# A hand-written list of small moves in the issue order of TensorE, ScalarE and VectorE, for a GLA and RWKV-7 inference step

## The chip, the cores and the metric

One core of one Trainium2 chip runs the whole program. The metric is device time in microseconds (us), the median of several executions. The engines are TensorE (PE; its weight loads are shown apart as PEld), VectorE (DVE), ScalarE (ACT), GpSimd (POOL) and SyncE (SP), which issues every DMA of this kernel. Each engine works through its own list of instructions in order, and waits on semaphores for the others.

## The reference

One layer of a hybrid decoder, for a prompt of 1024 tokens and for 8 single-token samples with stored states, width 1024, float32. Cut to what matters:

```python
p = einsum('btd,dn->btn', x, w_in)                    # one wide projection: GLA, RWKV and gate columns
# GLA branch, 4 heads: S_t = diag(a_t) S_{t-1} + k_t^T v_t ; o_t = q_t S_t   (chunked)
o_gla, S_gla = _gla_chunked(q, k, v, log_a, S_gla0)   # then RMS norm per head and a silu gate
# RWKV-7 branch, 16 heads of 64, per token:
# S_t = S_{t-1} (diag(w_t) - kk_t^T (kk_t * a_t)) + v_t^T k_t ; y_t = S_t r_t
y, S_rwkv = _rwkv7_scan(r, w, k, v, kk, a, S_rwkv0)   # then group norm, bonus term and a silu gate
m = sigmoid(gate_a) * (o_gla @ w_up_gla) + sigmoid(gate_b) * (o_rwkv @ w_up_rwkv)
y_out = layernorm(2**0.25 * x + m @ w_out)
```

It also returns both branches' states and the last projected row.

## The kernel before

The prompt is taken in two passes of 512 tokens; the first pass carries the 8 samples along. In each pass blocks of 128 columns of `w_in` are multiplied with x. A float32 product is made of three reduced-precision matmuls: weight and x are each split into a rounded part and a remainder (`wpart` and `xh`, `xl`), so that a block is 8 x 3 matmuls into a PSUM tile `proj` (the three `yield self.P.matmul(...)` in `blocks`). ScalarE or VectorE rounds a loaded weight piece (`CAST wpart<-wraw`), VectorE makes the remainder in the first pass; the second pass reads both kinds again from memory.

Between these blocks stand the two branches, each a generator that yields one operation at a time:

- `pair`: two RWKV heads at a time, eight per pass. `front` makes decays and products on ScalarE and VectorE; among the VectorE work are four half-height multiplies into the tile BK (rows `wide<-row 64x512`) and one `scalar_tensor_tensor` (r x rk x k), whose result `head_sums` splits into two `part` tiles and sums over each head with `headsr` on TensorE. After them come a triangular inverse on GpSimd (tiles X, Xt), and `back`, which assembles inverse blocks with four 32x32 transposes into `Xd` on VectorE and two groups of narrow matmuls, `big<-Xd,Ld` and `big<-Yd,Xt`, on quarters of the array.
- `chain`: the eight chunks of 64 tokens of a pair in sequence. Each chunk has three small float32 matmuls into the single bank `pch`: `pch<-wide,gg`, then `rh` (a copy) and `pch<-rh,XT`, a copy into u, then `pch<-wide`, and two 64x65 additions on VectorE (`wide<-pch,gg`, one for each head) that make the next chunk's u.
- `gla_head`: a GLA head (rows `big<-row ...`, narrow groups on 64x64 tiles among them, the copy S, the running state).

At the end come the two up-projections, the merge, the output product and the layer norm.

The order is not written by hand. `Order.run` keeps a model of five engines' times, and at each step takes the operation that can start first by it, less a priority (`PRIO`, `FOR_PE`, `TUNED`); the moment it is chosen, `op.fn()` issues it on its engine. Tiles are taken from pools (`take`) and given back (`free`) in the same order. Nearly all instructions are issued through `make` in class `Engine`, so that they all bear the line of its lambda (L283 in the profile of before, L316 after the change); the tiles tell them apart.

Of the kernel before, what the change touches and what calls it, by code (L numbers as in the profile page):

```python
# [20 lines left out]
P = 128  # L21
# [75 lines left out]
URGENT = 1.952  # L97

BOUNCED = (0, 1)

STRETCH = 5
TUNED = {
# [37 lines left out]
SIGMOID, EXP = "sigmoid_and_others", "natural_log_exp_and_others"  # L140
# [45 lines left out]
class Op:  # L186


    def __init__(self, ways, out, ins, lag=0.0, table=None, tiles=None, port=""):
        self.ways, self.out, self.ins, self.lag, self.table, self.tiles = ways, out, ins, lag, table, tiles  # L190
        self.port, self.outs = port, [out]
        self.eng, self.fn, self.cost = ways[0]
# [123 lines left out]
class Order:  # L316
# [4 lines left out]
    def __init__(self, nc):  # L321
        self.P, self.A, self.V, self.G, self.S, self.E, self.C = (Engine(**e) for e in (
            {"P": nc.tensor}, {"A": nc.scalar}, {"V": nc.vector}, {"G": nc.gpsimd}, {"S": nc.sync},
            {"V": nc.vector, "G": nc.gpsimd}, {"A": nc.scalar, "V": nc.vector}))
        self.tiles = (P, P)
        self.quads = {"V": {}, "A": {}}
        self.time = dict.fromkeys("PAVGS", 0.0)
        self.port = dict.fromkeys("VG", 0.0)
        self.dma = 0.0
        self.flight = [0.0] * FLIGHT  # L330
        self.table = EXP
        self.ready, self.read = {}, {}
        self.streams, self.stretch = [], None
        self.tune(0)
        self.idle, self.make, self.home, self.wait = {}, {}, {}, {}
        self.kept, self.tile = {}, {}

    def tune(self, n):
# [4 lines left out]
            self.for_pe = {k: max(0.0, FOR_PE.get(k, 0.0) + x.get("pe " + k, 0.0)) for k in PRIO}  # L343

    def buffers(self, tag, bufs, make):
        self.idle[tag], self.make[tag], self.wait[tag] = [0.0] * bufs, make, 0

    def fixed(self, tag, tiles):

# [19 lines left out]
    def take(self, tag):  # L369
        idle = self.idle[tag]  # L370
        t = min(idle)
        idle.remove(t)
        x = self.make[tag]()
        self.home[x.tensor.name] = tag
        if tag in self.kept:
            self.tile[x.tensor.name] = x
        self.ready[x.tensor.name] = (t, None)
        return x

    def free(self, *xs):  # L380
        for x in xs:
            n = x.tensor.name
            tag = self.home.pop(n)
            self.idle[tag].append(max(self.ready.pop(n)[0], self.read.pop(n, 0.0)))
            if tag in self.kept:
                self.kept[tag].append(self.tile.pop(n))

# [60 lines left out]
    def run(self):  # L448
        while self.streams:
            best, before = None, list(self.streams)  # L450
            self.urgent = self.needed()
            stand = max(STAND, SCARCE - PER_ROW * len(self.idle["row"]))
            for s in before:
                self.advance(s)
                if s.op is not None:
                    t = self.start(s.op)
                    if s.op.eng == "P":
                        key = t - stand * self.for_pe[s.kind] - (SWITCH if s.op.tiles != self.tiles else 0.0)
                    else:
                        key = t - self.prio[s.kind]  # L460
                    if s.kind in self.urgent:
                        key -= URGENT
                    if s.op.table not in (None, self.table):
                        key += max(0.0, TABLE - AGE * s.op.late)
                    if best is None or key < best[0]:
                        best = key, t, s
            if best is None:
                assert self.streams != before, "streams wait for one another"
                continue
            _, t, s = best  # L470
            op, s.op = s.op, None
            cost = op.cost
            if op.table not in (None, self.table):
                cost += TABLE
                self.table = op.table
                self.nc.scalar.preload_act_table_set(self.table)  # L476
            op.fn()
            self.time[op.eng] = max(self.time[op.eng], t + cost)
            if op.eng in op.port:
                self.port[op.eng] = t + cost  # L480
            if op.eng == "P":
                self.tiles = op.tiles
            elif op.eng in "VA":
                for x, q in self.starts(op):
                    self.quads[op.eng][x is op.out, x.space] = q
            end = t + cost
            if op.eng == "S":
                self.dma = max(self.dma, end) + op.lag[0]
                end = self.dma + op.lag[1]
                self.flight.append(end - EARLY)  # L490
            for x in op.outs:
                n = x.tensor.name
                self.ready[n] = max(end, self.ready.get(n, (0.0,))[0]), "D" if op.eng == "S" else op.eng
            for x in op.ins:
                n = x.tensor.name
                self.read[n] = max(self.read.get(n, 0.0), end)


class Kern(Order):
# [344 lines left out]
    def first_blocks(self, xs):  # L844

        run = []
        for b in self.plan[:2]:
            evac = yield from b.act()
            for tt, (t0, n) in enumerate(b.c.tiles):
                ps = yield from self.get("big")  # L850
                run.append((b, tt, t0, n, ps, evac))
        w, idle = {}, (yield from self.bank("pch", [P, P]))
        half = len(run) // 2
        for k, part in [(0, run[:half]), (1, run[:half]), (0, run[half:]), (1, run[half:])] + [(k, run) for k in range(2, NK)]:
            yield lambda: len(xs) > k
            for b, tt, t0, n, ps, evac in part:
                f0 = t0 - LEAD if b.lead and tt else t0
                q = ps[:, :t0 + n - f0]
                if tt == 0 and k % 4 == 0:
                    yield lambda: self.ws  # L860
                    w[id(b)] = self.ws.pop(0)
                hi, lo = (w[id(b)][:, v, k % 4 * P:k % 4 * P + P] for v in range(2))
                xh, xl = xs[k]
                yield self.P.matmul(q, hi, xh[:, f0:t0 + n], start=(k == 0), stop=False)
                yield self.P.matmul(q, hi, xl[:, f0:t0 + n], start=False, stop=False)
                yield self.P.matmul(q, lo, xh[:, f0:t0 + n], start=False, stop=(k == NK - 1))
                fin = tt == len(b.c.tiles) - 1
                if fin and k % 4 == 3:
                    yield from self.used(w[id(b)])
                if k == NK - 1:  # L870
                    self.spawn(self.evacuate(evac(tt, t0, n, q), ps, b.post if fin else None), "evacuate")
            for _ in range(IDLE if part is not run and part[0] is run[0] else 0):
                yield self.P.matmul(idle, self.warm, self.warm, start=True, stop=True)
            if k == 2:
                self.free(idle)
# [382 lines left out]
    def front(self, c, p, st, d):  # L1258
# [57 lines left out]
        self.free(ta, tb, te, td, r)  # L1316
        if c.i in BOUNCED:
            d.w = None
# [117 lines left out]
    def turn(self, c, d):  # L1436

        d.u = d.L.rearrange("p (c h v) -> p c h v", c=NCH, h=2)
        if c.i in BOUNCED:
            yield lambda: d.w is not None  # L1440
        m = yield from self.get("vm")
        if c.i in BOUNCED:
            w = d.w.rearrange("p (c v) -> p c v", v=C)
# [567 lines left out]
```

## Time and profile before

| | us |
|---|---|
| median of 3 runs (1435.57 to 1439.01) | 1437.1 |
| the profiled execution's own time | 1436.47 |
| its span, first to last instruction | 1434.7 |
| TensorE busy | 1415.7 |
| TensorE weight loads busy | 1245.6 |
| VectorE busy | 1071.1 |
| ScalarE busy | 871.8 |
| GpSimd busy | 414.1 |

The profiled execution is 0.6 us under the median. A matmul's recorded duration reaches past the start of the next one, since matmuls are pipelined; so the spacing of two starts tells what a matmul costs, and "idle before" in a row of the timeline counts only from the modelled end of the one before it.

### The profile page before, as it was taken

The numbers are of one execution on the slowest core, as the hardware profiler recorded it, in microseconds if no ns is written. First come the engines' busy times: TensorE is split into PE (matmuls) and PEld (weight loads), VectorE is DVE, ScalarE is ACT, GpSimd is POOL, SyncE is SP. The second block draws the span as 40 slices with busy tenths as digits, with TensorE's granted clock in tenths as the row PEclk, the third lists the DMA queues.
The fourth block names the chain that finished last, engine by engine and source line by source line (L and its number), as shares of the span: only waits on it lengthen the run. The fifth ranks groups of instructions, "written<-read, shape, count | busy, mean of one in ns | idle before, by whom it ended". The sixth has DMA issues, their size and how long they took to land.

```text
span 1434.7 us, 30718 instructions
## 1 busy us (share of the span) xinstructions
PE 1415.7 (99%) x10576; PEld 1245.6 (87%) x10576; DVE 1071.1 (75%) x2150; ACT 871.8 (61%) x2149; POOL 414.1 (29%) x1150
## 2 busy tenths in 40 slices
PE   9999999999999999999999999999999999999997
PEld 9999999999999998878788878888878897997786
DVE  7688688859886879563887888978785856676685
ACT  6556766666757667646575746586757655654210
POOL 1060524150624150505243514063414260000000
PEclk9999999999999999999999999999999999999999
DMA  7685977586867785688777778677677598798732
GB/s 262 182 261 149 269 220 218 137 244 202 237 179 209 243 264 173 172 239 245 230 207 210 196 242 215 182 218 214 173 230 228 174 273 260 246 302 284 256 126 81
DMA packets 341911, 310.26 MB, mean 216 GB/s; under 512 B 195411, under 2 KB 210908, under 8 KB 341756
## 3 DMA queue, kind: packets, MB, share of 16 engines
q1 hardware_dynamic: 341756, 308.31, 72.0%
q8 instruction: 84, 1.38, 0.4%
q14 instruction: 71, 0.58, 0.1%
HBM read 214.23 MB, written 92.92 MB: 214 GB/s over the span
## 4 chain that ended last, share of the span: by engine, by line
PE 89%; DVE 5%; ACT 4%; DMA 2%; issue 1%; SPq 0%; DVEq 0%; ACTq 0%
PE proj L283 57%; PE big L283 26%; PE pch L283 6%; ACT row L283 2%; DVE row L283 2%; DVE wide L283 1%; DMA wraw<-w_in 1%; ACT L476 1%; DMA wraw<-w_up_gla 1%; DVE wpart L283 1%; ACT wpart L283 0%; ACT part L283 0%; DVE az L283 0%; PE pch L600 0%; DVE xl L283 0%
## 5 line engine op out<-in xcount | busy, mean ns | idle before, releaser
L283 PE MATMUL proj<-xh,wpart 128*128 128x256 f32 (+3 forms) x3712 | 898.5, 327 | 3.4 <-DVE wpart L283 3.0
L283 PEld LDWEIGHTS proj<-xh,wpart 128*128 128x128 f32 x3712 | 617.2, 188 | 54.2 <-issue 4.6
L283 PE MATMUL proj<-xl,wpart 128*128 128x512 f32 (+3 forms) x1856 | 606.7, 327 | 0.2 <-DVE xl L283 0.2
L283 PEld LDWEIGHTS proj<-xl,wpart 128*128 128x128 f32 x1856 | 349.7, 188 | 26.6 <-issue 3.2
L283 POOL TENSOR_TENSOR Xt<-X,wide 128x60 f32<-128x60 f32 (+24 forms) x496 | 174.5, 352 | 413.5 <-DMA wide<-LD 245.6
L283 ACT CAST wpart<-wraw 128x512 fp32r<-128x512 f32 x298 | 182.3, 618 | 80.8 <-PE proj L283 31.3
L283 POOL TENSOR_TENSOR X<-X,Xt 128x60 f32<-128x60 f32 (+24 forms) x496 | 178.2, 359 | 38.6
L283 DVE TENSOR_TENSOR row<-row 128x512 f32<-128x512 f32 (+8 forms) x338 | 175.6, 530 | 10.2 <-ACT row L283 5.4
L283 DVE TENSOR_TENSOR wpart<-wraw,wpart 128x512 fp32r<-128x512 f32 x208 | 142.6, 696 | 44.5 <-ACT wpart L283 40.0
L283 ACT ACTIVATE row<-row 128x520 f32<-128x520 f32 (+4 forms) x229 | 138.0, 612 | 8.8 <-DMA row<-sg 3.3
L283 PE MATMUL big<-xh,wpart 128*128 128x256 f32 (+3 forms) x560 | 135.6, 328 | 0.4 <-ACT xh L283 0.4
L283 ACT COPY row<-big 128x128 f32<-128x128 f32 (+5 forms) x195 | 62.4, 341 | 65.1 <-PE big L283 61.4
L283 PEld LDWEIGHTS big<-xh,wpart 128*128 128x128 f32 x560 | 94.1, 189 | 8.5 <-ACT xh L283 0.8
L283 POOL TENSOR_TENSOR row<-row 128x512 f32<-128x512 f32 (+5 forms) x31 | 31.6, 1028 | 237.1 <-DVE row L283 116.4
L283 DVE TENSOR_TENSOR wide<-pch,gg 64x65 f32<-64x65 f32 x224 | 49.7, 222 | 63.1 <-PE pch L283 59.9
L283 PE MATMUL big<-xl,wpart 128*128 128x256 f32 (+3 forms) x280 | 91.4, 326 | 0.5 <-DVE xl L283 0.5
L283 ACT COPY rh<-pch 128x130 f32<-128x130 f32 x126 | 33.8, 268 | 95.2 <-PE pch L283 94.7
L283 DVE SCALAR_TENSOR_TENSOR row<-proj,pv,row 128x255 f32<-128x255 f32 (+1 forms) x95 | 54.4, 572 | 41.0 <-ACT tail L283 29.5
L283 ACT COPY wide<-pch 64x65 f32<-64x65 f32 x242 | 50.2, 207 | 42.2 <-PE pch L283 37.7
L283 PE MATMUL big<-row 128*64 128x64 f32 (+5 forms) x680 | 68.8, 287 | 0.0
L283 ACT ACTIVATE row<-proj,omu 128x256 f32<-128x256 f32 (+1 forms) x95 | 51.7, 545 | 26.6 <-PE proj L283 25.9
L476 ACT ACT_TABLE_LOAD x52 | 66.7, 1283 | 0.8
(221 smaller groups left out, 2049.5 us busy)
## 6 DMA issues: line engine op xcount, KB each, us to landing
wraw<-w_in SPq DMA_DIRECT2D x292, 256.0 KB
w<-wpart SPq DMA_DIRECT2D x146, 256.0 KB
wpart<-w SPq DMA_DIRECT2D x146, 256.0 KB
wide<-LD SPq DMA_DIRECT2D x64, 128.0 KB
BT<-row SPq DMA_DIRECT2D x32, 256.0 KB
wide<-BT SPq DMA_DIRECT2D x64, 128.0 KB
wraw<-w_up_gla SPq DMA_DIRECT2D x32, 256.0 KB
row<-w_out SPq DMA_DIRECT2D x32, 256.0 KB
```

What stands on the lines that cost most here:

```text
L283: ways.append((eng, lambda call=call: call(out, *args, **kw), price(eng, name, out, args, ins)))
L476: self.nc.scalar.preload_act_table_set(self.table)
```

## The change

The planner still runs as before, on the same numbers. But instead of issuing an operation when it chooses it, it appends it to a list (engine, function, tiles written, tiles read, activation table). For each tile taken from a pool it also notes which tile held that place before (`gone`, `follows`). When the plan is done, `issue` works out from the tiles which operations each one needs, makes one list for each engine, applies the table `MOVES` to the lists of TensorE ("P", 104 entries), ScalarE ("A", 58) and VectorE ("V", 99), and issues everything: always the operation that was planned earliest among those that stand first on their engine and have all they need issued. An entry (n, d) takes the operation at place n of its engine's list and puts it d places later (earlier where d is negative); entries apply one after the other. Without entries the issued program is that of before, instruction for instruction, with the same waits. The lists of GpSimd and SyncE have no entries, so the DMAs stand in the same order as before. No operation is added or removed, and the number of activation-table loads is the same (53).

```diff
+MOVES = {"P": [
+    (6, -4), (12, -2), (15, -4), (13, 2), (336, 9), (336, 8), (345, -1), (747, 4), (874, 3), (874, 5), (898, -11),
...
     def take(self, tag):
         idle = self.idle[tag]
         t = min(idle)
+        before = self.gone[tag].pop(idle.index(t))
         idle.remove(t)
         x = self.make[tag]()
+        self.follows[x.tensor.name] = before
...
-                self.nc.scalar.preload_act_table_set(self.table)
-            op.fn()
+            self.issued.append((op.eng, op.fn, {x.tensor.name for x in op.outs}, {x.tensor.name for x in op.ins}, op.table))
...
+        self.issue()
+
+    def issue(self):
+
+        todo = {e: [] for e in "PAVGS"}
+        wrote, read, touch, needs = {}, {}, {}, []
+        for n, (eng, _, outs, ins, _) in enumerate(self.issued):
+            todo[eng].append(n)
+            need = {wrote[x] for x in outs | ins if x in wrote}
+            for x in outs | ins:
+                if x in self.follows and x not in touch:
+                    need.update(touch.get(self.follows[x], ()))
+                touch.setdefault(x, []).append(n)
+            for x in outs:
+                need.update(read.pop(x, ()))
+                wrote[x] = n
+            for x in ins - outs:
+                read.setdefault(x, []).append(n)
+            needs.append(need)
+        for eng, moves in MOVES.items():
+            for n, places in moves:
+                todo[eng].insert(n + places, todo[eng].pop(n))
+        loaded, done, at = EXP, set(), dict.fromkeys(todo, 0)
+        while len(done) < len(self.issued):
+            n = min(todo[e][k] for e, k in at.items() if k < len(todo[e]) and needs[todo[e][k]] <= done)
+            eng, fn, _, _, table = self.issued[n]
+            if table not in (None, loaded):
+                loaded = table
+                self.nc.scalar.preload_act_table_set(table)
+            fn()
+            done.add(n)
+            at[eng] += 1
```

Three places show what the entries do. The numbers in the names of tiles differ between the programs, because after the change all tiles are made before the first instruction is issued; where a name is needed to follow, the sentences say which is which.

First, VectorE at 851 to 858 us of the profile of before, in the second pass. `wide_11134<-pch_12527` (after: `wide_1974<-pch_2222`) are a chunk's two additions, `wpart_12407` and `wpart_12506` (after: `wpart_2202` and `wpart_2216`) two weight pieces. Before:

```order
L283 TENSOR_TENSOR wide_11134<-pch_12527,gg_11136 64x65
L283 CAST wpart_12407<-wraw_12415 128x512
L283 CAST wpart_12506<-wraw_12511 128x512
L283 TENSOR_TENSOR wide_11134<-pch_12527,gg_11136 64x65
L283 STREAM_TRANSPOSE row_12538<-wide_12062 128x512
L283 SCALAR_TENSOR_TENSOR row_12544<-row_12545,row_12544 128x512
```

And after:

```order
L316 TENSOR_TENSOR wide_1974<-pch_2222,gg_1976 64x65
L316 CAST wpart_2202<-wraw_2204 128x512
L316 TENSOR_TENSOR wide_1974<-pch_2222,gg_1976 64x65
L316 STREAM_TRANSPOSE row_2223<-wide_2131 128x512
L316 CAST wpart_2216<-wraw_2218 128x512
L316 SCALAR_TENSOR_TENSOR row_2225<-row_2226,row_2225 128x512
```

The second cast moved two places later, behind the second addition and a transposition; the first cast still stands between the two additions.

Second, VectorE at 261 to 269 us, in the first pass. `wide_3888` (after: `wide_778`) is BK of a pair, `row_3925<-row_3472` (after: `row_788<-row_723`) the `scalar_tensor_tensor` of its `head_sums`, `part_4241` (after: `part_833`) the second of the two parts, `S_4186` (after: `S_823`) a GLA state. Before:

```order
L283 TENSOR_TENSOR wide_3888<-row_3924,row_3923 64x8x64
L283 STREAM_TRANSPOSE Xd0_184<-XT0_178 32x4x32 x4
L283 TENSOR_TENSOR wide_3888<-row_3585,row_3923 64x8x64
L283 SCALAR_TENSOR_TENSOR row_3925<-row_3472,pv_88,row_3585 128x512
L283 TENSOR_TENSOR wpart_4197<-wraw_4093,wpart_4197 128x512
L283 COPY S_4186<-big_4148 128x256
L283 TENSOR_TENSOR part_4241<-row_3925,part_4240 128x512
```

And after:

```order
L316 TENSOR_TENSOR wide_778<-row_787,row_786 64x8x64
L316 COPY S_823<-big_819 128x256
L316 STREAM_TRANSPOSE Xd0_184<-XT0_178 32x4x32 x2
L316 SCALAR_TENSOR_TENSOR row_788<-row_723,pv_88,row_737 128x512
L316 STREAM_TRANSPOSE Xd0_184<-XT0_178 32x4x32 x2
L316 TENSOR_TENSOR wide_778<-row_737,row_786 64x8x64
L316 TENSOR_TENSOR wpart_826<-wraw_811,wpart_826 128x512
L316 TENSOR_TENSOR part_833<-row_788,part_832 128x512
```

The `scalar_tensor_tensor` moved ahead of a multiply, and together with the copy S ahead of the last two of the four transpositions into Xd.

Third, TensorE at 548 to 552 us, where the pair's two narrow groups (`big<-Xd,Ld` and `big<-Yd,Xt`, 128x32 tiles of the array) and a GLA head's 64x64 products of `row` with itself (128x64 tiles) stand near each other. Before:

```order
L283 MATMUL big_8709<-Xd0_184,Ld_7748 32x128 x4
L283 MATMUL proj_8695<-xh6_317,wpart_8592 128x256
L283 MATMUL big_8740<-part_8684,headsr_154 128x512
L283 MATMUL proj_8695<-xl6_336,wpart_8592 128x256
L283 MATMUL proj_8695<-xh6_317,wpart_8592 128x256
L283 MATMUL proj_8695<-xh7_335,wpart_8592 128x256
L283 MATMUL big_8735<-Yd0_182,Xt_8733 32x128 x4
L283 MATMUL proj_8695<-xl7_384,wpart_8592 128x256
L283 MATMUL proj_8695<-xh7_335,wpart_8592 128x256
L283 MATMUL big_8740<-part_8685,headsr_154 128x512
L283 MATMUL big_8759<-row_7894 64x64 x4
L283 MATMUL big_8759<-row_7896 64x64 x4
```

And after:

```order
L316 MATMUL proj_1539<-xl7_240,wpart_1527 128x256
L316 MATMUL proj_1539<-xh7_234,wpart_1527 128x256
L316 MATMUL big_1548<-part_1537,headsr_154 128x512
L316 MATMUL big_1541<-Xd0_184,Ld_1389 32x128 x4
L316 MATMUL big_1550<-row_1414 64x64 x4
L316 MATMUL big_1550<-row_1416 64x64 x4
L316 MATMUL big_1550<-row_1471 64x64 x4
L316 MATMUL big_1546<-Yd0_182,Xt_1545 32x128 x4
L316 MATMUL proj_1549<-xh0_200,wpart_1522 128x266
```

The first narrow group moved behind the block's remaining matmuls, and the second behind the GLA head's groups: the three stand in one row now, with no full-array matmul between them. Over the whole program the list of TensorE changes the shape of its array tiles 219 times before and 211 times after.

More of the change, by code (lines that the diff above doesn't have):

```diff
@@ L332, in __init__ @@
         self.ready, self.read = {}, {}
-        self.streams, self.stretch = [], None
+        self.streams, self.stretch, self.issued = [], None, []
         self.tune(0)
-        self.idle, self.make, self.home, self.wait = {}, {}, {}, {}
+        self.idle, self.make, self.home, self.wait, self.gone, self.follows = {}, {}, {}, {}, {}, {}
         self.kept, self.tile = {}, {}
@@ L345, in buffers @@
     def buffers(self, tag, bufs, make):
-        self.idle[tag], self.make[tag], self.wait[tag] = [0.0] * bufs, make, 0
+        self.idle[tag], self.make[tag], self.wait[tag], self.gone[tag] = [0.0] * bufs, make, 0, [None] * bufs
     def fixed(self, tag, tiles):
@@ L384, in free @@
             self.idle[tag].append(max(self.ready.pop(n)[0], self.read.pop(n, 0.0)))
+            self.gone[tag].append(n)
             if tag in self.kept:
```

30 rows, old and new, of the table MOVES are left out of this document.

## The prediction

> **What bounds the kernel now.** I read the page's busy times, clock and chain first, then the table by stretches, the waits of TensorE, and at each long wait the timeline of TensorE and of the engine it waited for.
>
> ```profile
> PE 1415.7 (99%) x10576; PEld 1245.6 (87%) x10576; DVE 1071.1 (75%) x2150; ACT 871.8 (61%) x2149; POOL 414.1 (29%) x1150
> ...
> PEclk9999999999999999999999999999999999999999
> ...
> PE 89%; DVE 5%; ACT 4%; DMA 2%; issue 1%; SPq 0%; DVEq 0%; ACTq 0%
> ...
> L283 PEld LDWEIGHTS proj<-xh,wpart 128*128 128x128 f32 x3712 | 617.2, 188 | 54.2 <-issue 4.6
> ```
>
> TensorE is busy 99% of the span at full clock in all 40 slices, and the chain that ended last runs through it for 89%. An order that leaves the instructions as they are can only win what TensorE stands still, and what its changes of form cost. The next rows (busy us of PE, PEld, DVE, ACT, POOL by stretch) bound the first:
>
> ```profile
> 1427.00:1434.70 7.70, 0.01 (x1) 0.00 (x0) 4.38 (x9) 0.50 (x2) 0.00 (x0) 0.72 0.19 68
> sum 1434.70, PE 1415.71 PEld 1245.56 DVE 1071.06 ACT 871.76 POOL 414.06; mean PE 157.30 PEld 138.40 DVE 119.01 ACT 96.86 POOL 46.01
> ```
>
> Of 1434.7 - 1415.7 = 19.0 us without a matmul 7.7 are the tail behind the last one, which the table does not touch. The rest is in TensorE's waits (sum, number, longest):
>
> ```profile
> PE proj L283 <- DVE wpart L283: 3.0, 3, 1.8
> PE big L283 <- ACT part L283: 2.8, 4, 1.0
> PE pch L283 <- DVE wide L283: 1.8, 3, 0.9
> ...
> PE big L283 <- DVE xl L283: 0.5, 2, 0.3
> PE big L283 <- DVE S L283: 0.4, 1, 0.4
> PE proj L283 <- DVE row L283: 0.4, 2, 0.2
> PE big L283 <- ACT xh L283: 0.4, 1, 0.4
> PE proj L283 <- DVE xl L283: 0.2, 1, 0.2
> PE big L283 <- DVE gg L283: 0.2, 1, 0.2
> ```
>
> Eighteen stops, 9.7 us. A stop costs more than its idle time, since that counts only from the modelled end of the matmul before:
>
> ```profile
> 855.86 0.40 PE L283 MATMUL proj<-xl,wpart 128*128 128x512 f32 x1
> 856.09 0.39 PE L283 MATMUL proj<-xh,wpart 128*128 128x512 f32 x1
> 857.37 0.46 PE L283 MATMUL pch<-wide,gg 128*128 128x130 f32 x2 [0.89 <-DVE wide L283]
> ...
> 686.08 0.63 PE L283 MATMUL proj<-xh,wpart 128*128 128x512 f32 x2
> 687.29 0.50 PE L283 MATMUL big<-part,headsr 128*128 128x512 f32 x1 [0.58 <-ACT part L283]
> 687.63 0.40 PE L283 MATMUL proj<-xl,wpart 128*128 128x512 f32 x1
> ```
>
> Undisturbed, 512 columns follow each other every 0.23 us (855.86 to 856.09), so the next was due at 856.32 and came 1.05 late, 0.16 more than the 0.89 shown. Behind a stop the next start comes 0.34 instead of 0.23 later (687.29 to 687.63). I add 0.28 to each stop: all eighteen are worth 9.7 + 18 x 0.28 = 14.7 us, 1% of the time. The Trainium skill, "Perfetto Trace Analysis", section "Identifying the Most-Contended Engine", holds matmul busy time a bad measure of a TensorE's headroom and names the busy share of weight loads instead; by its measure 13% of the span, some 187 us (an estimate from the 87% above), would be open. The pitch of 0.23 decides here: a 512-column matmul outlasts its weight load of 0.188, so weight loads idle there though nothing waits.
>
> **The change, part by part.** No instruction and no DMA is added or dropped; SyncE's and GpSimd's lists stand as they were. So each term is a stop that goes, stays or comes.
>
> (1) The three `pch` stops on VectorE's additions: the additions move ahead of what held them. The rows of VectorE at one of them:
>
> ```profile
> 851.39 0.22 DVE L283 TENSOR_TENSOR wide<-pch,gg 64x65 f32<-64x65 f32 x1 [0.58 <-PE pch L283]
> 853.62 0.44 DVE L283 CAST wpart<-wraw 128x512 fp32r<-128x512 f32 x1 [2.01 <-DMA wraw<-w_in]
> 856.53 0.43 DVE L283 CAST wpart<-wraw 128x512 fp32r<-128x512 f32 x1 [2.47 <-DMA wraw<-w_in]
> 856.99 0.23 DVE L283 TENSOR_TENSOR wide<-pch,gg 64x65 f32<-64x65 f32 x1
> ```
>
> The two additions read the same `pch`. The first ran at 851.39; the second stood behind two casts that waited for their DMAs, until 856.99, and TensorE stopped for it. After the change only the first cast is ahead of it: it ends by 853.62 + 0.44 + 0.23 = 854.3, two us before 856.32. The second cast waits for its DMA as before, behind an addition and a transposition that are done by 855. Gain of the three: 1.8 + 3 x 0.28 = 2.6.
>
> (2) The four stops on `part`, where a pair's `head_sums` waits for its `scalar_tensor_tensor`. The table moves that ahead of multiplies in all four; the rows of VectorE at 687, and TensorE and VectorE at 404:
>
> ```profile
> 684.82 2.43 DVE L283 SCALAR_TENSOR_TENSOR row<-row,pv 128x512 f32<-128x512 f32 x2
> ...
> 404.56 0.50 PE L283 MATMUL big<-part,headsr 128*128 128x512 f32 x1 [0.98 <-ACT part L283]
> ...
> 403.77 1.28 DVE L283 TENSOR_TENSOR wpart<-wraw,wpart 128x512 fp32r<-128x512 f32 x2
> 404.97 0.69 DVE L283 TENSOR_TENSOR part<-row,part 128x512 fp32r<-128x512 f32 x1
> ```
>
> At 687 it passes two multiplies, more than a us of work, and the second `part` is asked for five matmuls later than before: 0.58 + 0.28 = 0.86, all gained. The stop of 0.44 at 829 is alike: 0.72. At 404 the first half comes in time, but the second `part` (404.97 to 405.66) keeps nearly all of VectorE's work ahead of it, only one weight remainder (1.28 / 2 = 0.64) passes behind: 0.64 of the 1.26. The last is the place of the second order piece:
>
> ```profile
> 265.35 0.43 PE L283 MATMUL big<-Xd,Ld 128*32 128x128 f32 x8
> ...
> 268.45 0.50 PE L283 MATMUL big<-part,headsr 128*128 128x512 f32 x1 [0.80 <-ACT part L283]
> ...
> 264.64 0.62 DVE L283 STREAM_TRANSPOSE Xd<-XT 32x128 f32<-32x128 f32 x2
> 265.29 1.69 DVE L283 TENSOR_TENSOR wide<-row 64x512 f32<-64x512 f32 x1
> 267.00 0.75 DVE L283 SCALAR_TENSOR_TENSOR row<-row,pv 128x512 f32<-128x512 f32 x1
> ```
>
> Here the moved 0.75, and the copy S, stand ahead of the last two transpositions, which end at 265.26 before and some 1.2 later now; TensorE needs them at 265.35. The stop of 0.80 goes, one of about 1.1 comes 3 us earlier. I count zero. Together 0.86 + 0.72 + 0.64 = 2.2.
>
> (3) Five small stops have entries at their place: `xh` and one `big` `xl` at 1292 us, where four matmuls of the next tile fill the gap; one `row`, the `proj` `xl`, and `gg`. 0.4 + 0.3 + 0.2 + 0.2 + 0.2 + 5 x 0.28 = 2.7.
>
> (4) What stays: the three `wpart` stops (3.0 + 0.84), since the casts they wait for wait themselves for a DMA (853.62 above), and DMAs keep their order. The `S` stop at 1119 us and the other `xl` and `row` stops at 1133 to 1135 lie in a stretch in which VectorE has no slack:
>
> ```profile
> 1117.00:1134.00 17.00, 16.34 (x118) 12.54 (x117) 16.12 (x27) 13.08 (x30) 5.00 (x3) 1.00 0.62 185
> ...
> 1075.41 0.50 PE L283 MATMUL proj<-xh,wpart 128*128 128x512 f32 x1 [0.97 <-DVE wpart L283]
> ```
>
> It is busy 16.12 of 17.0 us, and no entry carries work out past 1134; a us won at 1119 is waited for again at 1133. Zero.
>
> (5) TensorE's changes of array form, 219 to 211. Rows at the third order piece:
>
> ```profile
> 548.49 0.28 PE L283 MATMUL proj<-xh,wpart 128*128 128x256 f32 x1
> 548.70 0.42 PE L283 MATMUL big<-Xd,Ld 128*32 128x128 f32 x8
> 549.05 0.39 PE L283 MATMUL proj<-xh,wpart 128*128 128x256 f32 x1
> 549.27 0.40 PE L283 MATMUL big<-part,headsr 128*128 128x512 f32 x1
> ```
>
> A 256-column matmul takes 0.12 to the next start in a row of its kind (half of the 0.23 of 512); on the way into the narrow group it is 0.21, and the first one behind the group takes 0.22. A trip out and back costs 0.09 + 0.10 = 0.2. At this place three trips become one; over the program eight changes go: at least 0.8 (each half a trip), at most 8 trips or 1.6, since a change between two narrow forms may cost less than one to and from the full array. I take 1.6: the counts of changes from and to the full array fall by eight each.
>
> (6) New stops. Of the nine places that I followed one by one, one traded its stop for another (268) and one kept half (404). The other two hundred entries are unread; the same may happen there. Two more stops of mean size, 14.7 / 18 = 0.82, make -1.6. Bounds: none, or every gain of (1) to (3) given back, -7.5.
>
> Sum: 2.6 + 2.2 + 2.7 + 1.6 - 1.6 = 7.5 us off the profiled execution's 1436.5, 1429.0. That execution is 0.6 under the median, so for the median 1429.5, 0.5% faster.
>
> **The rivals.** More is won: no new stops, 404 and 268 in full (another 1.7), and the many one-place moves saving something that my stops don't show: 11 to 15 us, 1422 to 1426. The stop at 268, read closely, speaks against it.
>
> Half is given back: VectorE and ScalarE do the same work in total, and where they are dense (1117 to 1134) an earlier operand only means a later other one. 3 to 4 us stay, 1433.5. For it: one in four of the `part` stops already comes to nothing. Against: VectorE is idle a quarter of the span.
>
> Nothing is won: TensorE comes sooner to the weight pieces, and the next late DMA takes back what was gained since the one before. All but what lies behind 1152 us, the last `wpart` stop, would go: 1435 to 1436. Against: a load is issued when TensorE has freed a buffer, so the loads come sooner too.
>
> It is slower: an operation moved forward waits at the head of its engine's list, and holds all behind it, as the two casts above held an addition. At 1075 us an entry puts just such a cast, which TensorE waits for, ahead of a copy out of PSUM. The price of one is the 2.0 to 2.5 us of those casts' waits, if TensorE needs what is behind. To come out slower by 0.2% it takes (7.5 + 2.9) / 2.5, four or five that TensorE feels. The Trainium skill's "TensorE: Matmul & The Clock Gate", section "Architectural detail: the array is 16× 32×32, not 1× 128×128", says that VectorE's and ScalarE's queues are strictly first in, first out. By that rule the trace agrees: the addition of 856.99 had its operand before 851.39 and did not overtake.
>
> **How the numbers follow.** No change means within 0.2% of 1437.1 (2.9 us, what a measurement of this kernel can tell), 1434.2 to 1440. The forecast, 1427 to 1432, has 0.50; more won 0.15; half given back, 1432 to 1434.2, 0.20; nothing won 0.09; slower 0.06. Faster is 0.50 + 0.15 + 0.20 = 0.85. The range from 1423 to 1436 leaves out the slower case, half of the unchanged one and the lower end of the second: below 0.2.
>
> **What would show it.** The page would have TensorE's busy time nearly the same and the span some 7 us shorter. In the waits of TensorE `DVE wide` would be gone and `ACT part` under 1.5, `DVE wpart` still near 3. At the second order piece's place TensorE would wait for the transpositions into Xd instead of for `part`. At the third, the narrow groups would follow each other without a full-array matmul between. I would be wrong if `DVE wpart` grew by what the others lost (nothing won), or if new rows such as `Xd` added up to more than 3 us (given back).

## The result, and the profile after

The changed kernel took 1426.7 us (median of six executions, 1424.0 to 1430.4) beside 1436.5 for the kernel before (median of six, 1435.6 to 1439.0): ratio 0.9933, 95% interval 0.9912 to 0.9954. Run again in the first experiment it came to 0.9948 (0.9934 to 0.9962). So 0.5 to 0.7% is won, 7.5 to 9.7 us; forecast were 7.5. The profiled execution is a long one: 1430.4 us, span 1428.6, 6.1 us shorter than the span before.

The busy times and the chain, the row of the tail (the last 7.9 us, columns as in the stretches of the prediction), and the waits of TensorE:

```profile
PE 1410.7 (99%) x10576; PEld 1245.5 (87%) x10576; DVE 1072.7 (75%) x2150; ACT 870.9 (61%) x2149; POOL 418.2 (29%) x1150
...
PE 89%; DVE 4%; DMA 3%; ACT 2%; issue 1%; SPq 1%; DVEq 0%; ACTq 0%
...
1420.70:1428.60 7.90, 0.22 (x2) 0.02 (x1) 4.37 (x9) 0.50 (x2) 0.00 (x0) 0.75 0.19 66
...
PE proj L316 <- DVE wpart L316: 3.2, 2, 2.5
PE pch L316 <- DVE wide L316: 1.9, 2, 1.3
PE pch L316 <- ACT rh L316: 1.2, 2, 1.0
...
PE big L316 <- DVE part L316: 0.7, 2, 0.5
PE pch L316 <- ACT row L316: 0.6, 1, 0.6
PE big L316 <- issue: 0.3, 1, 0.3
PE big L316 <- DVE gg L316: 0.3, 1, 0.3
PE pch L316 <- ACT wide L316: 0.2, 1, 0.2
PE big L316 <- DVE sto L316: 0.2, 1, 0.2
PE proj L316 <- DVE row L316: 0.2, 1, 0.2
```

The tail is as it was. The waits without the warm-up's 1.1 us fell only from 9.7 to 8.8 us, while the span fell by 6.1: most of the old stops are gone (the four on `part` too; the two stops on `part` that are there now, 0.7 together, are at other places), others have come, and the longest is longer. The rest of the gain lies where this view shows nothing, since TensorE's modelled busy time (1415.7, now 1410.7) covers every delay too short to count as idle.

A view that counts all of it is worked out from the starts of matmuls in the traces: the start of the n-th matmul before, less that of the n-th in the other kernel, is the lead at that place (median over 24 starts). The table has what the lead gained over a stretch of the kernel before; "changed" is the execution above, e1 to e9 are the experiments below:

```
us of before changed   e1    e2    e3    e4    e5    e6    e9
200-212        0.75  0.74  0.73  0.07  0.10  0.08  0.08  0.08
262-275        1.12  1.12 -2.68  1.12 -0.02 -0.04  0.33  1.09
286-300        0.47  0.47  0.48 -0.04 -0.01  0.00 -0.20  0.00
325-345        0.90  0.90  0.55  0.73  0.53  0.50  0.24  0.50
345-375       -1.32 -0.25 -0.74  0.13 -0.66  0.05 -0.03 -0.16
395-416        1.04  1.04 -0.02  0.89  0.22  0.46  0.28  0.61
465-485       -0.80 -0.83 -0.00 -0.80 -0.85  0.00  0.00  0.00
680-691        0.69  0.70 -0.52  0.83  0.09 -0.57  0.47  0.64
700-735       -1.01 -0.49 -0.38 -1.05 -1.68  0.25  0.35 -1.60
820-846        0.68  0.69 -0.35  0.03  0.01  0.01  0.03  0.01
846-862       -1.08  1.49 -0.64  1.49 -1.27  1.11  1.15  1.49
1070-1082     -0.31  0.39  0.15  1.21  0.11 -0.47 -0.47  0.06
1112-1130      0.97  0.97 -0.01  0.97  0.23  0.99 -0.19  0.80
1130-1156      0.10 -0.89 -0.08 -0.31  0.08  0.07 -4.65 -1.02
1156-1175      0.76  0.76 -0.47  0.38  0.76  0.76  0.00  0.79
1232-1245      0.36  0.33  0.36 -0.00  0.36  0.01  0.00  0.00
1280-1300      1.22  1.22  1.22  0.01  0.57  0.00  0.01  0.01
elsewhere      1.55  0.24  0.39  2.66  1.19 -1.07  1.08  0.16
all            6.08  8.60 -2.02  8.32 -0.25  2.12 -1.53  3.45
```

Most steps repeat to 0.03 us in each kernel that has the same entries (262-275, 1112-1130). Others differ between two executions of one program (345-375, 846-862, 1070-1082): there TensorE waits for something behind a transfer. The last row is also the difference of the spans. Cut into stretches of 25 us throughout, the profiled execution won 11.9 us and lost 5.9 again (14.6 and 8.5 in stretches of 10 us, where matmuls that only change places count as well).

The kernel before, too, is here in a single execution, and its own luck stands in every column. e7 and e10 below show how much: e7 has entries at 479 and 693 us only, and "gains" 1.24 at 846-862; e10 moves no matmul and nothing on ScalarE or VectorE, and "gains" 0.59 at 1156-1175. At 1130-1156 the two lose 0.79 and 0.97, with nothing moved there. So the steps at these three places do not by themselves speak for or against an entry.

### The profile page after: what moved, and what is told of

Same layout as the page of the kernel before. It is cut to its first block, busy times and chain, and to the rows that moved or that the text cites. A ratio compares the mean times of both kernels' runs of the same rounds, so it can differ in the third digit from the quotient of the medians.

```text
span 1428.6 us, 30711 instructions
## 1 busy us (share of the span) xinstructions
PE 1410.7 (99%) x10576; PEld 1245.5 (87%) x10576; DVE 1072.7 (75%) x2150; ACT 870.9 (61%) x2149; POOL 418.2 (29%) x1150
## 4 chain that ended last, share of the span: by engine, by line
PE 89%; DVE 4%; DMA 3%; ACT 2%; issue 1%; SPq 1%; DVEq 0%; ACTq 0%
PE proj L316 57%; PE big L316 26%; PE pch L316 6%; DMA wraw<-w_in 2%; DVE row L316 2%; ACT row L316 1%; SPq L316 1%; DVE wide L316 1%; DVE gg L316 0%; DMA w<-wpart 0%; DMA row<-o_gla 0%; DVE part L316 0%; DVE wpart L316 0%; PE pch L667 0%; DVE XT L316 0%
## 5 line engine op out<-in xcount | busy, mean ns | idle before, releaser
L316 POOL TENSOR_TENSOR Xt<-X,wide 128x60 f32<-128x60 f32 (+24 forms) x496 | 178.6, 360 | 410.7 <-DMA wide<-LD 268.4
```

The lines of the kernel that those rows point to most:

```text
L316: ways.append((eng, lambda call=call: call(out, *args, **kw), price(eng, name, out, args, ins)))
```

## The experiments

Each ran beside the kernel before. All times come from these ratios; the table above shows one profiled execution of each, which can be some us off the median.

| | kernel | ratio | 95% interval | us faster |
|---|---|---|---|---|
| e1 | the changed kernel again | 0.9948 | 0.9934 to 0.9962 | 7.5 |
| e2 | only the entries at the places of (1) to (3) | 0.9993 | 0.9982 to 1.0004 | 1.0 |
| e3 | all the others | 0.9953 | 0.9940 to 0.9967 | 6.7 |
| e4 | only TensorE's table | 0.9996 | 0.9985 to 1.0006 | 0.6 |
| e5 | of the entries of e3, only VectorE's | 0.9986 | 0.9976 to 0.9996 | 2.0 |
| e6 | of the entries of e3, only ScalarE's | 0.9999 | 0.9988 to 1.0010 | 0.1 |
| e7 | two pieces of TensorE's table alone | 0.9999 | 0.9987 to 1.0012 | 0.1 |
| e8 | the changed kernel without them | 0.9941 | 0.9927 to 0.9955 | 8.5 |
| e9 | of the entries of e3, VectorE's and ScalarE's | 0.9966 | 0.9953 to 0.9980 | 4.9 |
| e10 | before, six loads issued earlier | 0.9983 | 0.9971 to 0.9995 | 2.4 |
| e11 | e8 with these loads | 0.9928 | 0.9911 to 0.9945 | 10.3 |
| e12 | e11 with three copies of a chain ahead | 0.9919 | 0.9905 to 0.9933 | 11.6 |

**e1, unaltered.** 

> The changed kernel once more, unaltered. Its first three executions took 1428.7 to 1430.4 us, the next three 1424.0 to 1424.8. Theory L (late data): the difference is made by stops behind transfers and behind what waits for them, which fall differently from execution to execution; the profiled one lost 2.49 us in one stop on a weight piece at 850 us and then some 1.8 us in matmuls at about half rate until 855. An execution near 1424 then shows that stop under 2 us and no slow matmuls behind it. Rival C: the same stops, and a lower rate spread over the whole span; then the two executions keep their distance in all stretches. Time expected by both: 1424 to 1431 us.

1425.1 to 1430.2 us, profiled at 1427.9. Theory L holds, though no execution near 1424 was profiled: most steps are those of the first execution, and the two differ where transfers are waited for, most of all at 846-862 (+1.49 against -1.08). TensorE in the first execution, and the stretch:

```profile
847.42 0.40 PE L316 MATMUL big<-alr,gw 128*128 128x512 f32 x1
850.30 0.50 PE L316 MATMUL proj<-xh,wpart 128*128 128x512 f32 x1 [2.49 <-DVE wpart L316]
...
850.87 0.69 PE L316 MATMUL proj<-xh,wpart 128*128 128x512 f32 x2
...
851.36 0.63 PE L316 MATMUL proj<-xl,wpart 128*128 128x512 f32 x1
851.79 1.05 PE L316 MATMUL proj<-xh,wpart 128*128 128x512 f32 x2
852.64 0.63 PE L316 MATMUL proj<-xl,wpart 128*128 128x512 f32 x1
...
850.00:855.00 5.00, 4.70 (x15) 3.79 (x16) 3.39 (x6) 2.85 (x5) 4.09 (x12) 0.66 0.93 318
```

The load was not late against before (its cast ended 3.8 us sooner), but TensorE came 4.5 us sooner (847.42 instead of 851.89 for the matmul ahead of the stop); and 1.1 us behind the stop 512 columns take 0.43 us instead of 0.23 (851.36 to 851.79), at a granted clock of 0.66 in these 5 us. In e1 the same stop was 0.94 us, with no slow matmuls behind it.

**e2 and e3, the places and the rest.** The table was cut at places where the order before and after hold the same operations; e2 keeps 29 of these blocks, e3 the others.

```diff
-MOVES = {"P": [
-    (6, -4), (12, -2), (15, -4), (13, 2), (336, 9), (336, 8), (345, -1), (747, 4), (874, 3), (874, 5), (898, -11),
...
+MOVES = {
+    "P": [(1435, -8), (1435, -2), (1438, -4), (2319, -1), (2320, -1), (2321, -1), (2327, -3), (2328, -3), (2329, -2),
...
```

> Only the entries at the places of terms (1) to (3): 71 single moves in 29 blocks of the three lists; every other place stands as before. Theory M (the forecast): the stops named carry the gain, so this is worth 2.6 + 2.2 + 2.7 = 7.5 us, less little for new stops: 1429 to 1431 us beside 1436.5 for the kernel before, and 0 to 3 us slower than the changed kernel. Rival S (spread): the many small moves elsewhere carry a good part; then this wins less than half of what the changed kernel wins.

> The complement: all entries except those at the places of terms (1) to (3). Theory M: +1.6 for array forms, -1.6 for new stops, zero for the rest: within 2 us of the kernel before. Rival S: 3 to 6 us faster than before. In the trace of the changed kernel the stretch from 1119 to 1166 us, which the forecast put at zero, gave 1.8 us; if that is no luck of one execution, it shows here too.

Theory M falls: the entries at the places I had read are worth 1.0 us, the others 6.7, as much as the whole table within the intervals. The column of e2 shows it place by place: 206, 289, 1239 and 1292 us go as forecast, and so does the stop at 829 (0.68 won there, 1.0 lost at 844 on a transfer); 687 and 268 us are worse than before, the latter with half-rate matmuls behind its stop. VectorE and TensorE in e2 at 268, then VectorE in the changed kernel:

```profile
260.16 3.08 DVE L295 TENSOR_TENSOR wide<-row 64x512 f32<-64x512 f32 x3
263.25 0.42 DVE L295 COPY S<-big 128x256 f32<-128x256 f32 x1
263.69 0.61 DVE L295 STREAM_TRANSPOSE Xd<-XT 32x128 f32<-32x128 f32 x2
264.32 1.87 DVE L295 SCALAR_TENSOR_TENSOR row<-row,pv 128x512 f32<-128x512 f32 x1
266.22 0.62 DVE L295 STREAM_TRANSPOSE Xd<-XT 32x128 f32<-32x128 f32 x2
...
266.90 0.42 PE L295 MATMUL big<-Xd,Ld 128*32 128x128 f32 x8 [2.25 <-DVE Xd L295]
...
258.70 0.69 DVE L316 TENSOR_TENSOR wide<-row 64x512 f32<-64x512 f32 x1
260.12 0.42 DVE L316 COPY S<-big 128x256 f32<-128x256 f32 x1 [0.73 <-ACT row L316]
260.56 0.61 DVE L316 STREAM_TRANSPOSE Xd<-XT 32x128 f32<-32x128 f32 x2
261.18 0.75 DVE L316 SCALAR_TENSOR_TENSOR row<-row,pv 128x512 f32<-128x512 f32 x1
261.97 0.62 DVE L316 STREAM_TRANSPOSE Xd<-XT 32x128 f32<-32x128 f32 x2
```

The order at the place is the same, and in e2 it does what the prediction said: the last transpositions come late, by 2.25 us even, since the moved operation took 1.87 us. In the changed kernel they end at 262.6, 4.2 us earlier, while TensorE is only 1.3 us earlier there than in e2. VectorE even stands idle there (0.73). And e3, which has none of these moves at 264 to 269 us, has the same +1.12. What takes the stop away lies elsewhere. By the order of the lists I take it to be the entries at 244 to 262 us of before: on ScalarE an activation of the pair goes ahead of others, and on VectorE a `scalar_tensor_tensor` of the pair ahead of a weight remainder; both feed the multiplies into BK. No run holds these entries alone, so which of the others do it is not shown.

**e5, e6 and e9, which engine's.**

```diff
-MOVES = {"P": [..., "A": [..., "V": [...
...
+MOVES = {"A": [(237, -1), (253, -3), (256, -1), (321, -1), ...], "V": [(61, -1), ...]}
```

The lines are those of e9; e5 has its second list alone, e6 its first.

> Of the entries away from the forecast's places (all of them together: 7.4 us faster) only VectorE's: 146 single moves. The stops at 268, 337, 404, 687, 854 and 1119 us went without an entry at their place. Theory U (upstream): entries 10 to 30 us ahead let VectorE and ScalarE reach the place earlier relative to TensorE; nearly all of these are VectorE's, so this alone gives over half: 4 to 6 us faster, with + 1.1 at 262 to 275 and + 1.0 at 1112 to 1130. Rival T (together): at 268 us ScalarE's moves at 256 to 259 feed VectorE's; then VectorE's alone give less than 2.5 us and nothing at 262 to 275.

> Of the same entries only ScalarE's: 86 single moves. Theory U: under 1.5 us faster. Rival T: also under 1.5 us, since each needs the other. If ScalarE is what held VectorE back (rival A), 3 us or more faster.

> VectorE's and ScalarE's entries away from the forecast's places, both together, TensorE's list as before. Apart they gave 2.0 and 0.1 us, with TensorE's and together 6.7. Theory T (together): the stops go only where ScalarE hands over earlier and VectorE takes it earlier: 4 to 6 us faster, with + 1.1 at 262 to 275, + 0.6 at 395 to 409, + 0.8 at 680 to 691. Rival P: TensorE's entries are the third part that is needed; then 2 us as the sum of the two, and no + 1.1 at 262 to 275.

Theory T: apart 2.0 and 0.1 us, together 4.9. At 268 us VectorE's entries alone give nothing, ScalarE's 0.33, both 1.09; at 687 us -0.57, 0.47 and 0.64. With TensorE's part of e3 the three make 6.7 (TensorE's whole table alone gives 0.6, e4). The parts don't add up to the whole; by the ratios alone e9 lies 2.8 us above the sum of e5 and e6, about as much as their intervals allow, and it is the steps at 268 us that show it. The -4.65 of e6 at 1130-1156 is a case of the slow matmuls told below.

**e4, TensorE's table alone.**

```diff
-MOVES = {"P": [..., "A": [..., "V": [...
...
+MOVES = {"P": [(6, -4), (12, -2), (15, -4), ...]}
```

> Only TensorE's table, ScalarE's and VectorE's lists as before. Theory M: the array forms (1.6), and of the stops those at which TensorE's own list puts other matmuls ahead (206, 337, 714, 1239 and 1292 us: up to 0.8, 0.5, 0.6, 0.5 and 1.3): 2 to 5 us faster. Rival W: an operand that comes late stops TensorE wherever the matmul stands, as its list moves by a few matmuls of 0.12 to 0.23 us each; then only the array forms stay, 0.8 to 1.6 us.

0.6 us by the ratio, less than either theory's 2 or 0.8. The array forms are there: at 160-180, 760-790, 890-912 and 975-988 us the lead grows by 0.20 to 0.22 in e4 as in the changed kernel, e1 and e3, and not in e5, e6 and e9, which lack TensorE's entries. It is the 0.2 of one trip. But the same table loses 0.85 at 479 us and 1.68 at 700-735.

**e7 and e8, two harmful pieces.**

```diff
+MOVES = {"P": [(3318, -2), (3318, -1), (4426, -1), (4427, -1), (4428, -1), (4429, -1), (4430, -1)]}
```

> The kernel before with only two pieces of TensorE's table: at 479 us a pch product is put ahead of a group of sixteen narrow products (the changed kernel stands 0.57 us there for its operand), and at 693 us such a group is put behind five block matmuls. Theory Q (a queue passed on): the group's result comes 1.1 us later, SyncE's transfers that need it too, and with them all that SyncE issues behind them, so that a weight piece is late at 713 us. Expected: 0.8 slower at 465 to 485 and 1 to 1.7 slower at 700 to 735, nothing elsewhere: 2 us slower in all. Rival: the stops at these places belong to other entries or to chance; then there is no step at either.

> The changed kernel without these two pieces. Theory Q: 0.8 back at 465 to 485 and 0.5 to 1 at 700 to 735: 1.3 to 1.8 us faster than the changed kernel, ratio to the kernel before 0.9935. Rival: no difference from the changed kernel (0.9948).

TensorE at the first piece in the changed kernel:

```profile
474.08 0.29 PE L316 MATMUL proj<-xh,wpart 128*128 128x264 f32 x1
474.94 0.46 PE L316 MATMUL pch<-wide,gg 128*128 128x130 f32 x2 [0.57 <-ACT row L316]
475.33 0.93 PE L316 MATMUL big<-az,wide 64*128 64x128 f32 x11
```

The narrow group that used to fill this gap was put behind. The step of -0.8 is in every kernel that has the piece (-0.81 in e7) and in none without it (-0.01 in e8): shown. The second piece is not: e7 lost 0.62 at 700-735 instead of 1 to 1.7, and e8 still lost 0.85 there. As times neither kernel differs clearly: the 2 us expected of e7 do not show in its ratio, and e8 lies 1.0 us below e1 with overlapping intervals. One step of 0.8 is less than the spread of the stops behind transfers.

**e10 to e12, the late weight pieces.** SyncE's list before, and the cast that last read the place in memory which the load at 850.37 fills:

```profile
834.73 1.14 ACT L283 CAST wpart<-wraw 128x512 fp32r<-128x512 f32 x2
...
836.38 2.71 SPq L283 DMA_DIRECT2D row<-VT  x4
839.13 2.19 SPq L283 DMA_DIRECT2D wide<-Sp  x2
841.41 0.53 SPq L283 DMA_DIRECT2D wpart<-w  x1
...
842.51 1.98 SPq L283 DMA_DIRECT2D LD<-gg  x4
844.53 3.28 SPq L283 DMA_DIRECT2D Ld<-gg  x4
...
848.55 1.77 SPq L283 DMA_DIRECT2D wide<-LD  x4
850.37 0.42 SPq L283 DMA_DIRECT2D wraw<-w_in  x1
```

The place is free at 835.9 at the latest, and the load is issued 14 us later, behind more than twenty other transfers, most of them a pair's, that SyncE issues one by one. A load waits for SyncE here, not for a buffer. Its issue was 3.7 us earlier in e8, where TensorE was 5.0 us ahead. So moves on the other engines make such a stop shorter or longer and do not take it away: at this matmul it was 0.54 to 3.48 us in all eleven traces with SyncE's list as before, and it is gone in e10, e11 and e12.

```diff
+MOVES = {"S": [(848, -14), (850, -8), (1031, -13), (1033, -7), (1302, -15), (1304, -8)]}
```

> The kernel before with six moves in SyncE's list alone: at three places two weight loads are issued 7 to 15 places earlier, ahead of the transfers of a pair, since their buffers are free 15 to 17 us before they are issued (852, 1072 and 708 us). Theory Q: SyncE's list makes the weight pieces late; the wpart stops of 1.83 and 0.97 us go, and the 0.89 behind the first: with 0.28 each 4.5 us faster, +3.2 at 846 to 862, +1.2 at 1070 to 1082. Rival D: the DMA engines (fully busy from 845 to 860) are the bound, and the load lands as late; under 1 us. A loss is possible if the pair's transfers, 0.4 to 0.9 us later, reach GpSimd too late.

> The changed kernel without the two harmful pieces of TensorE's table, and with these six moves in SyncE's list. Its wpart stops were 0.55 to 3.5 us at 848 us (with half-rate matmuls behind the long ones), and 0.6 to 1.3 at 709 and 1070. Theory Q: + 2 to 4 us against the kernel without the six moves (1427.4): 1423 to 1425.5, ratio 0.9915 to 0.993. Rival D: no change, 1427.

The two `wpart` stops at the places of the moves (854 and 1075 us) go, so theory Q holds on the cause; on the size it was wrong, 2.4 us instead of 4.5, and 1.8 more than e8 in e11 where 2 to 4 were expected. Rival D fails: the DMA engines' share was 0.42, 0.82 and 0.99 in the three stretches of 5 us from 845 us of before (0.94 and 0.98 in the first two in e8), so they were not full when the load could have gone. What is late next took the place of the two, and one of 0.68 us came on a weight piece at 1152 us, where nothing is moved. TensorE's waits in e10, TensorE at 856 us, and ScalarE there:

```profile
PE pch L287 <- ACT rh L287: 2.9, 2, 1.5
...
PE proj L287 <- ACT wpart L287: 0.7, 1, 0.7
...
PE proj L287 <- DVE wpart L287: 0.2, 1, 0.2
...
856.27 0.49 PE L287 MATMUL pch<-rh,XT 128*128 128x130 f32 x2 [1.49 <-ACT rh L287]
...
853.38 1.28 ACT L531 ACT_TABLE_LOAD   x1
854.68 0.63 ACT L287 ACTIVATE row<-row 128x512 f32<-128x512 f32 x1
855.34 0.72 ACT L287 ACTIVATE row<-row,b_one 128x512 f32<-128x512 f32 x1
855.97 0.25 ACT L287 COPY rh<-pch 128x130 f32<-128x130 f32 x1
```

The chain's copy stands behind a table load and two activations, which the wait for the weight had covered before; a second stop like it came at 1078 us. In e11 the same stop was 1.49 us. e12 takes the copy ahead:

```diff
-        ..., (2035, -1), (2036, -1), (2037, -1)],
+        ..., (2035, -1), (2036, -1), (2037, -1), (595, -1), (1381, -2),
+        (1741, -1)],
```

> The kernel of e11 with three more moves in ScalarE's list: a chain's copy rh goes ahead of two activations at 849 us (where TensorE stood 1.49 us for it once the weight piece came in time) and of a weight cast at 363 us (0.68) and at 1069. Theory U (what is late next): TensorE's stop goes to whatever stands ahead in a list; with rh free, + 1.5 at 846 to 862 and + 0.7 at 360 to 375: 2 us faster than e11, ratio to the kernel before 0.991 to 0.992. Rival: another operand is as late there (a weight cast behind it), and nothing is won: 0.9928.

1424.3 us, ratio 0.9919: the fastest kernel here, faster than the one before, and beside e1 its interval (0.9905 to 0.9933) ends just below that of the changed kernel (0.9934 to 0.9962); it overlaps that of the first measurement. The stops on `rh` are gone, at 363 us with 1.5 us gained (345-375: 0.13 after -1.42 in e11), but at 846-862 nothing was added (1.16 after 1.47): TensorE now waits 1.03 us one step further on:

```profile
853.25 0.49 PE L339 MATMUL pch<-wide 128*128 128x130 f32 x2 [1.03 <-ACT wide L339]
```

That is the rival's case there; of the 2 us expected over e11, 1.3 came, within the intervals.

## Why the prediction was right, and where it was not

The time came out (1426.7 in a range of 1423 to 1436, 2.8 below the forecast; 1428.2 when run again), but by two errors that nearly cancel, and that they do is luck. The terms foresaw 9.1 us won and 1.6 lost to new stops; the profiled pair shows some 12 won and 6 lost; in e1 the balance is 8.6. One of the forecast's own signs of being wrong did appear: waits of kinds that the list of before does not have add up to 3.2 us in the first profile (1.2, 0.7, 0.6, 0.3, 0.2 and 0.2), over the 3 that were to mean "given back", though in e1 they are 1.8. The wait for Xd that was to appear is in neither.

(1) The `pch` stops: at 206 us 0.75 came for the 0.82 counted. At 714 the stop went, but one of 0.7 on a weight piece 3 us ahead came, and 700-735 lost 1.0 and 0.5. The stop at 857 went; but e5, e6 and e7, without its entry, gained 1.1 to 1.2 there too: the stop on the weight piece ahead, 1.83 us in the one execution of before, was 0.54 to 1.12 in them. So of 2.6 us some 0.8 are safe.

(2) The `part` stops: 0.69 at 687 and 0.68 at 829 for 0.86 and 0.72; at 404 1.04 instead of 0.64, at 268 1.12 instead of zero. The step that failed: I read what passes what at the place, with operands at the times of before. All but 829 went also in e3, without those entries, and with them alone, in e2, nothing was won at the three. The credit belongs to entries elsewhere, which I had left unread and counted at zero but for two new stops; at 268 and 687 us it is ScalarE's and VectorE's together (e9: 1.09 and 0.64).

(3) The small stops: 0.47, 0.90, 0.36 and 1.22 where 2.7 in all was forecast: right. Here the entries at the place do it (e2: 0.48, 0.55, 0.36, 1.22), but for 337, where the others give as much (e3: 0.73). At 1292 the gain is twice the idle time that the waits had shown (0.37 and 0.31), as 0.28 for each stop had it.

(4) What was to stay: wrong at 1119 (+0.97), where I had argued from VectorE's 16.12 busy us of 17.0. VectorE is no less dense in the changed kernel (16.40 of 17.0 us from 1113.5 on) and yet comes to the awaited operation sooner (e5, its entries alone: 0.99). That it is waited for again further on, as I had argued, is not shown: 1130-1156 lost 0.9 in e1, but as much in e7 and e10. `wpart` stayed, as said, at 3.2 us in the waits of the first profile, but not steadily: 2.4 in e1 and 0.8 in e3, by how far the load was ahead of TensorE. e10 shows why it stays.

(5) The array forms: 0.21 for a trip as worked out, in four stretches and at 691-700; these five trips are 1.1 of the 1.6 counted. At the third order piece, where two more trips go, nothing is seen in the lead: TensorE's `part` product there starts 0.40 us behind a 256-column matmul that leads by 0.12, so 0.28 of the saved 0.4 is a delay that no wait row names (in e4, at the same matmul, one does: 0.36 us for `part`):

```profile
545.14 0.28 PE L316 MATMUL proj<-xh,wpart 128*128 128x256 f32 x1
545.54 0.49 PE L316 MATMUL big<-part,headsr 128*128 128x512 f32 x1
545.97 0.43 PE L316 MATMUL big<-Xd,Ld 128*32 128x128 f32 x8
```

(6) New stops: 1.6 counted, some 6 lost. I took two of mean size; there were thirteen new or longer ones, the largest at 363, 475, 571, 709, 850, 960 and 1075 us of the profiled execution (0.49 to 2.49 us), and the one at 850 brought the half clock. This is the term that was sized wrong by most.

Of the rivals, "more is won" had the larger gains right, and the full gain at 268 that I had held against it; "half is given back" had the mechanism of the loss. "Nothing is won" named the right cause of the losses, late transfers, but the loads did come sooner, by 3.8 of TensorE's 4.5 us at 850. They did so for another reason than the one I had held against this rival, that a load is issued when TensorE has freed a buffer: the buffer at 850 was free for 14 us, and the load came sooner because SyncE reached it sooner. The slower case's mechanism stands in the trace, at 1075 us, where a cast waited 2.25 us for its load ahead of two additions:

```profile
1074.55 0.43 DVE L316 CAST wpart<-wraw 128x512 fp32r<-128x512 f32 x1 [2.25 <-DMA wraw<-w_in]
1074.89 0.45 DVE L316 TENSOR_TENSOR wide<-pch,gg 64x65 f32<-64x65 f32 x2
...
1075.49 0.46 PE L316 MATMUL pch<-wide,gg 128*128 128x130 f32 x2 [1.31 <-DVE wide L316]
```

It cost 0.3 us there against before, where a stop of 0.97 stood at the same place; in e3 and e8, with the same entry, that place gained 1.21.

Open stays whether the whole table gains more than e3 (7.5 and 9.6 us by its two ratios, beside 6.7): the entries of e2 add 3.5 us of steady steps to it in the traces (206, 289, 829, 1239, 1292), and the ratios of e1 and e3 differ by 0.7 us with intervals of 2 us to either side. Whether later stops take these back or the medians hide them, these runs don't tell.

## What to carry to other kernels

Here a stop was set by the slowest of all lists that led to it, so the entries at the place said little: subtract the places from the change and run both halves before you believe a sum. Count a reordering in the lead of the n-th start, not in the waits, and expect that what is won in front of a transfer is kept only as far as the list that issues the transfer runs ahead too. When a wait is taken away, look up what the waiting had covered on the other engines; it is the next stop.

## What was not expected of the hardware

In this case TensorE fell to half rate behind stops of about 2.4 us and more. In the fourteen traces all five single stops of 2.45 us or more between two starts (2.45 and 2.54 in e2, 2.88 in the changed kernel, 3.06 in e4, 3.87 in e8) are followed by 512-column matmuls at 0.427 us, or by 256-column ones at 0.22, some of them after a us at full rate; stops of up to 2.23 (the one at 854 us before) are not. In e6 three stops of 0.93, 0.35 and 0.85 us idle within 3 us did the same. In the clock records of these traces the granted clock is 0.50 for 3.4 us each time, in e6 for 6.8. Granted clock by stretch in e8 and in e6 (the column behind the five engines):

```profile
850.00:855.00 5.00, 4.26 (x14) 3.47 (x15) 3.44 (x6) 2.09 (x5) 4.14 (x12) 0.66 0.98 308
...
1130.00:1135.00 5.00, 3.22 (x16) 2.66 (x17) 5.00 (x8) 2.45 (x7) 2.47 (x6) 0.81 0.74 235
1135.00:1140.00 5.00, 5.00 (x25) 5.00 (x25) 2.58 (x6) 1.58 (x4) 0.00 (x0) 0.51 0.09 16
```

At 0.20 us more for each matmul, the six or seven that are slow in the changed kernel cost an estimated 1.3 us on top of the stop. A stop that grew from 1.8 to 2.5 us idle so cost 2 us, not 0.7. The Trainium skill, "TensorE: Matmul & The Clock Gate", section "HAM oscillation — how this bites in real kernels", warns of idle gaps of more than some 3.4 us. By the granted 0.50 it is the half-rate state that this section of the Trainium skill tells of; but the shortest gap that brought it on here was 2.45 us, and the measurement decides.
